# Attention's output projection by seven block products, one weight sum formed by an accumulating transfer

## The chip, the cores and the metric

One core of a Trainium2 chip runs the kernel. The metric is device time in microseconds (us), the median of several runs of the same kernel; lower is better. Engines are named as the profile names them: PE is TensorE's matmul, PEld its weight loads, DVE is VectorE, ACT is ScalarE, POOL is GpSimd, and SP issues most DMAs. L1286 is line 1286 of the kernel before.

## The reference

One inference step of a one-layer trunk over T = 520 token columns (512 of a prompt, 8 decode tokens), model width 2048, everything in float32:

```
y = mixer(rmsnorm(x)); x += y @ w_out          # two recurrent head groups
q = rmsnorm(x) @ w_cq                          # 4 heads of 512, 256 memory tokens
o = softmax(q mk^T / sqrt(512)) mv
x += o @ w_co                                  # 2048 x 2048: attention's output projection
x += relu(rmsnorm(x) @ w_up)^2 @ w_down        # 2048 -> 8192 -> 2048
out = rmsnorm(x)
```

The decode tokens attend to their own cached K and V. The change is about `o @ w_co`.

## The kernel before

Activations lie transposed, 128 features by 520 tokens in a block; a 2048-wide activation is 16 blocks. Every float32 operand is split into a rounded high part and the remainder; a product is three matmuls, high by high, high by low, low by high. A matmul takes a 128 x 128 piece of weights and 260 tokens. Weights come in tiles of 128 x 1024 (512 KB); a "job" is what PE does with one such tile.

The work is a list of jobs run by `run_jobs`. While job i is emitted, the tile of job i+2 is split (ACT writes `whi`, L129 or L138; DVE subtracts to make `wlo`, L130 or L146), tiles further ahead are loaded, and every background task (`start`, `step_tasks`) takes a step. `whi` and `wlo` have three buffers each, so a split waits for the end of the job three before it. In some ranges (`manual_schedule`) each engine keeps the order in which the code was written; elsewhere a planner orders instructions by priority and by its own costs. The attention part and the first four jobs of the w_co projection are in such a hand-ordered range.

Two ways of multiplying are used. `gemm` is the plain one: 48 matmuls a job, and 32 jobs for a 2048 x 2048 projection. `quad_jobs` takes a 2 x 2 arrangement of weight tiles A11, A12, A21, A22 and does seven products in place of eight, each of 24 matmuls. DVE forms four sums of tiles for a group of seven: S3 = A11 - A21, S1 = A21 + A22, S2 = A11 - S1 and the operand of P3, A12 - S2 (L1256). The activations need combinations too: blocks 4 to 7 of an activation pair are made by four DVE subtractions (`block_sums`, L1195, or in `y_sums`), split, and partly parked in DRAM for later loads. Before, w_out (the mixer's projection), w_up and w_down use `quad_jobs`: w_out as one plain pair of output blocks (`out_plain`, four jobs) and seven groups (`out_quad`, 49 jobs). Here w_co is a plain `gemm` over 16 output blocks through `residual`: 32 jobs.

Attention ends per head in `attn_prompt`. The products p @ mv (L222) come four to a head; ACT and DVE split each into `oh`, `ol` (L1159, L1160), which w_co reads. Between them run the jobs that make memory keys and values (`mk_jobs`, L1050; `mv_jobs`, L1081), and the decode tokens' attention, which DVE does by long multiply-reduce instructions (L962, L969) on K and V streamed over POOL's queue (L930, L937).

`residual` loads the old x from DRAM, adds PSUM (L871), stores the new x, and calls `fact_out`, which at once makes the split operands of w_up (`fa`, L800, L801) and the four block combinations, spread over the projection's 16 outputs. `block_loads` then brings the parked ones back. w_up starts with four plain jobs (`up_plain`, L1329), then groups of seven (L1286).

Of the kernel before, what the change touches and what calls it, by code (L numbers as in the profile page):

```python
# [9 lines left out]
F32 = mybir.dt.float32  # L10
F32R = mybir.dt.float32r
# [34 lines left out]
def tile_trunk(ctx: ExitStack, tc: tile.TileContext, a, o):  # L46
# [9 lines left out]
    early_pools = ctx.enter_context(ExitStack())  # L56
    small = early_pools.enter_context(tc.tile_pool(name="small", bufs=2))
    pmm = early_pools.enter_context(tc.tile_pool(name="pmm", bufs=2, space=PSUM))
    paux = early_pools.enter_context(tc.tile_pool(name="paux", bufs=4, space=PSUM))
# [744 lines left out]
    def y_out(t, n):  # L804
        fy[n] = [pair_slot("fy") for _ in range(2)]
        for hf in range(2):
            split_to(fy[n][hf], t[:, HALF[hf]])
        if n % 2 == 0:
            y_even[n // 2] = t
        else:  # L810
            start(y_sums(n // 2, y_even.pop(n // 2), t))

    def y_sums(i, t0, t1):

        yield
        r = stream((P, 4, HT))
        b12, b11, b21, b22 = t0[:, HALF[1]], t0[:, HALF[0]], t1[:, HALF[0]], t1[:, HALF[1]]
        for k, p, q in ((0, b12, b11), (2, b22, r[:, 0]), (1, b22, b12), (3, b21, r[:, 2])):
            V.tensor_tensor(out=r[:, k], in0=p, in1=q, op=ALU.subtract)
        if i >= len(ydram):  # L820
            ykept[i] = {j: r[:, j - 4] for j in range(4, 8)}
            return
        yield
        hi = small.tile([P, 4, HT], F32R, tag="kv", name=nm("kv"), bufs=7)
        S.copy(hi, r)  # L825
        V.tensor_tensor(out=r.bitcast(F32R), in0=r, in1=hi.bitcast(F32), op=ALU.subtract)
        for b, x in enumerate((hi.bitcast(F32), r)):
            load(ydram[i][:, :, b].rearrange("j p c -> p j c"), x)
# [29 lines left out]
    def residual(wname, acts, src, dst, key, out, then=None):  # L858
        js = []
        for n in range(KB):  # L860
            box = {}

            def pre(n=n, box=box):
                box["x"] = xr_tile()
                load(box["x"], src[n])

            def ev(ps, n=n, box=box):
                if n == 0:
                    st[key] = slot(key)
                x1 = slot("x1")  # L870
                V.tensor_tensor(out=halves(x1), in0=ps, in1=halves(box["x"]), op=ALU.add)  # L871
                load(dst[n], x1)
                out(x1, n)
                add_sq(st[key], x1, n == 0)
                if n == KB - 1:
                    start(rstd_task(key))
                    if then:
                        then()
            js += gemm([a[wname][n, g] for g in range(2)], acts, ev, pre)
        return js  # L880


    SC = 512.0 ** -0.5
    xatt, oact = [None] * KB, []
# [210 lines left out]
    def attn_prompt(h):  # L1095
# [57 lines left out]
        ops = []  # L1153
        for j in range(6):
            if j >= 2:
                op = ops.pop(0)
                hi, lo = slot("oh", dt=F32R), slot("ol", dt=F32R)
                for src, c in ((op, slice(0, TP)), (od[:, 4 * h + j - 2], DEC)):
                    S.copy(hi[:, c], src)  # L1159
                    V.tensor_tensor(out=lo[:, c], in0=src, in1=hi[:, c].bitcast(F32), op=ALU.subtract)  # L1160
                oact.append((hi, lo))
# [40 lines left out]
    put_off = []  # L1202

    def fact_out(x1, n):
        if "sb" not in late:
            put_off.append((x1, n))
            return
        fact[n] = [pair_slot("fa") for _ in range(2)]
        for hf in range(2):
            split_to(fact[n][hf], x1[:, HALF[hf]], pc(C_FFN, n))  # L1210
        i, kp = divmod(n, 2)
        if kp == 0:
            tkept[i] = late["sb"].tile([P, 8, HT], F32, tag="r", name=nm("r"), bufs=2)
        r = tkept[i]
        if kp:
            S.activation(r[:, 2:4], halves(x1), AF.Copy, scale=pc(C_FFN, n))
            block_sums(r)
            if i < len(td):
                start(sums_out(tkept.pop(i), i))
            else:  # L1220
                tkept[i] = {j: r[:, j] for j in range(4, 8)}
        else:
            for hf in range(2):
                S.activation(r[:, 1 - hf], x1[:, HALF[hf]], AF.Copy, scale=pc(C_FFN, n))
# [10 lines left out]
    def quad_jobs(srcs, acts, nacc, evac, order=None, early=False):  # L1235
# [82 lines left out]
    def plain_pair(srcs, facts, post):  # L1318
# [3 lines left out]
        def mm(mp, kp, wh, wl):  # L1322
            if kp == 0:
                ps[mp] = mm_tile()
            for j in range(8):
                x = facts[2 * j + kp]
# [29 lines left out]
    x1 = [None] * KB  # L1356

    def x1_load(m):
        for n in (2 * m, 2 * m + 1):
            x1[n] = slot("x1") if m else xr_tile()  # L1360
            load(x1[n], a["xT"][n])

    def x1_done(n):
        load(dx[0][n], x1[n])
        if n == 0:
            st["ssx"] = slot("ssx")
        add_sq(st["ssx"], x1[n], n == 0)
        if n == KB - 1:
            start(rstd_task("ssx"))
        if n >= KB - 2:  # L1370
            xatt[n] = split(x1[n], "xa", pc(C_X, n))

    def x1_again():

        raw = {}
        for n in range(0, KB, 2):
            for k in (n, n + 1):
                if k < KB - 2:
                    raw[k] = slot("x1")
                    load(raw[k], dx[0][k])  # L1380
            if n:
                for k in (n - 2, n - 1):
                    xatt[k] = split(raw.pop(k), "xa", pc(C_X, k))
            yield

    def out_plain():
        def post(mp, ps):
            V.tensor_tensor(out=halves(x1[mp]), in0=ps[:, :, 0:HT], in1=halves(x1[mp]), op=ALU.add)
            x1_done(mp)
            if mp:  # L1390
                x1_load(1)
        js = plain_pair(a["w_out"][0], fy, post)
        js[0]["pre"] = lambda: x1_load(0)
        js[1], js[2] = js[2], js[1]
        return js

    def out_quad(m):
        def evac(p, ps):
            n, hf = dict(P1=(0, 0), P2=(0, 0), P6=(0, 1), P5=(1, 1), P7=(1, 1), P3=(0, 1), P4=(1, 0))[p]
            x = x1[2 * m + n][:, HALF[hf]]  # L1400
            V.tensor_tensor(out=x, in0=ps[:, 0, 0:HT], in1=x, op=ALU.add)
            if p == "P5" and m + 1 < KB // 2:
                x1_load(m + 1)
            if p in ("P3", "P4"):
                x1_done(2 * m + n)
            if p == "P4" and m == KB // 2 - 2:
                start(x1_again())
        return quad_jobs([a["w_out"][m, mp, kp] for mp in range(2) for kp in range(2)],
                         lambda p: [ty[k][PLACE[p]] for k in range(KB // 2)], 1, evac, early=True)
# [151 lines left out]
    jobs += out_plain()  # L1561
    for m in range(1, KB // 2):
        jobs += out_quad(m)
# [11 lines left out]
    jobs += residual("w_co", oact, dx[0], dx[1], "ssf", fact_out, lambda: start(block_loads(tact, fact, td, tkept), 2.0))  # L1575
    jobs[n_early + 1], jobs[n_early + 2] = jobs[n_early + 2], jobs[n_early + 1]
# [21 lines left out]
    early_pools.close()  # L1598
    late["sb"] = ctx.enter_context(tc.tile_pool(name="late", bufs=2, reuse_waits="tile"))
    late["mm"] = ctx.enter_context(tc.tile_pool(name="lmm", bufs=3, space=PSUM, reuse_waits="tile"))  # L1600
    late["aux"] = ctx.enter_context(tc.tile_pool(name="laux", bufs=2, space=PSUM, reuse_waits="tile"))
    for x1, n in put_off:
        fact_out(x1, n)
# [6 lines left out]
def _pack(i):  # L1610
# [6 lines left out]

    i = {k: np.asarray(v) for k, v in i.items()}
    f = np.float32
    par = np.zeros((P, NPAR), f)  # L1620
    for base, name in ((C_MIX, "g_mix"), (C_X, "g_xattn"), (C_FFN, "g_ffn"), (C_FIN, "g_final"),
# [33 lines left out]
        w_out=i["w_out"][0].reshape(8, 2, P, 8, 2, P).transpose(3, 4, 1, 2, 0, 5), w_cq=gran(i["w_cq"][0]), w_co=gran(i["w_co"][0]),  # L1655
        w_up=i["w_up"][0].reshape(8, 2, P, 32, 2, P).transpose(3, 4, 1, 2, 0, 5),
# [49 lines left out]
```

## Time and profile before

| | us |
|---|---|
| median of 3 runs | 2667.88 (2666.63 to 2674.22) |
| profiled execution | 2668.74 |
| its span, first to last instruction | 2667.0 |
| PE busy | 2639.8 |
| DVE busy | 2135.2 |
| ACT busy | 1253.2 |
| granted TensorE clock | 0.998 of full speed |

A busy time is the sum over an engine's instructions. Instructions of one engine overlap a little, so spacing between starts is shorter than the durations shown. The chain of waits is the profile's list, in order of time, of what each moment of the span was spent on, followed back from the last instruction.

### The profile page before, as it was taken

How to read it: one execution, taken by the hardware profiler on the slowest of the kernel's cores; microseconds unless marked ns; L12 is line 12 of the kernel's file. 1: busy time of each engine (PE TensorE's matmuls, PEld its weight loads, DVE VectorE, ACT ScalarE, POOL GpSimd, SP SyncE). 2: the span in 40 equal slices, each digit the busy share in tenths (PEclk: the TensorE clock that was granted, in tenths of full speed). 3: DMA queues.
4: the chain of work that ended last, by engine and by line, in shares of the span. 5: the costliest groups of instructions: out<-in, count | busy, mean ns of one | idle time of the engine just before them, and what ended most of it. 6: DMA issues, size and time to landing. Idle time of an engine off the chain costs nothing.

```text
span 2667.0 us, 52574 instructions
## 1 busy us (share of the span) xinstructions
PE 2639.8 (99%) x21418; PEld 2602.9 (98%) x21418; DVE 2135.2 (80%) x3593; ACT 1253.2 (47%) x1704; POOL 108.3 (4%) x184
## 2 busy tenths in 40 slices
PE   9999999999999999999999999999999999999997
PEld 9999999999999999989999999999999999999997
DVE  6786786897865567775569999999999998998898
ACT  5646364553453144444445555555553333333344
POOL 0010000000001212110000000000000000000001
PEclk9999999999999999999999999999999999999999
DMA  5354443566456778775566565565579666555642
GB/s 205 105 191 135 124 162 105 177 220 235 141 180 200 274 264 279 264 243 192 184 226 228 195 211 196 190 210 198 189 245 335 217 219 219 180 172 191 212 131 89
DMA packets 236068, 528.91 MB, mean 198 GB/s; under 512 B 24638, under 2 KB 96990, under 8 KB 235826
## 3 DMA queue, kind: packets, MB, share of 16 engines
q1 hardware_dynamic: 216882, 458.43, 51.1%
q0 software_dynamic: 18944, 67.12, 7.3%
q8 instruction: 168, 2.75, 0.4%
q14 instruction: 74, 0.61, 0.1%
HBM read 426.27 MB, written 99.33 MB: 197 GB/s over the span
## 4 chain that ended last, share of the span: by engine, by line
PE 91%; issue 4%; DVE 2%; DMA 2%; ACT 1%; POOL 0%; SPq 0%; POOLq 0%; DVEq 0%; ACTq 0%
PE mm L1286 46%; PE mm L203 29%; PE mm L1050 3%; PE mm L1081 3%; PE aux L222 3%; PE aux L1286 2%; PE mm L1329 2%; DVE wlo L130 1%; PE aux L657 1%; DMA wraw<-in_w_in 1%; PE aux L728 0%; PE aux L661 0%; DMA hc<-r 0%; PE aux L654 0%; DMA wraw<-in_w_mv 0%
## 5 line engine op out<-in xcount | busy, mean ns | idle before, releaser
L129 ACT CAST whi<-wraw 128x1024 fp32r<-128x1024 f32 x396 | 416.0, 1051 | 730.1 <-PE mm L1286 388.2
L1286 PE MATMUL mm<-ha,whi 128*128 128x260 f32 x3584 | 643.5, 283 | 1.9 <-ACT whi L129 1.0
L130 DVE TENSOR_TENSOR wlo<-wraw,whi 128x1024 fp32r<-128x1024 f32 x396 | 483.1, 1220 | 151.3 <-ACT whi L129 149.2
L1286 PEld LDWEIGHTS mm<-ha,whi 128*128 128x128 f32 x3584 | 551.0, 188 | 2.8 <-DVE X L1455 1.3
L1286 PE MATMUL mm<-ha,wlo 128*128 128x260 f32 x1792 | 505.0, 282 | 0.6 <-DVE wlo L130 0.6
L1286 PE MATMUL mm<-ta,whi 128*128 128x260 f32 x2320 | 419.3, 283 | 0.0
L1286 PEld LDWEIGHTS mm<-ta,whi 128*128 128x128 f32 x2320 | 356.2, 188 | 0.0
L1286 PEld LDWEIGHTS mm<-ha,wlo 128*128 128x128 f32 x1792 | 337.0, 188 | 1.0 <-DVE wlo L130 1.0
L1286 PE MATMUL mm<-ta,wlo 128*128 128x260 f32 x1160 | 326.8, 282 | 0.0
L1286 PE MATMUL mm<-fa,whi 128*128 128x260 f32 x1488 | 268.3, 282 | 0.0
L203 PE MATMUL mm<-xh,whi 128*128 128x260 f32 x1280 | 264.2, 287 | 0.9 <-DVE og L775 0.9
L203 PE MATMUL mm<-xl,whi 128*128 128x260 f32 x1280 | 259.9, 284 | 0.0
L203 PE MATMUL mm<-xh,wlo 128*128 128x260 f32 x1280 | 257.8, 282 | 0.0
L1286 PEld LDWEIGHTS mm<-fa,whi 128*128 128x128 f32 x1488 | 228.1, 188 | 0.0
L129 ACT CAST whi<-A 128x1024 fp32r<-128x1024 f32 x126 | 132.3, 1050 | 185.6 <-PE mm L1286 120.2
L138 ACT CAST whi<-wraw 128x1024 fp32r<-128x1024 f32 x100 | 105.1, 1051 | 243.5 <-PE mm L203 84.6
L1286 PEld LDWEIGHTS mm<-ta,wlo 128*128 128x128 f32 x1160 | 218.4, 188 | 0.0
L1286 PE MATMUL mm<-fa,wlo 128*128 128x260 f32 x744 | 209.2, 281 | 0.0
L1455 DVE TENSOR_TENSOR X<-mm,X 128x260 f32<-128x260 f32 x448 | 170.6, 421 | 41.4 <-PE mm L1286 39.5
L203 PEld LDWEIGHTS mm<-xh,whi 128*128 128x128 f32 x1280 | 198.4, 188 | 2.3 <-ACT kv L825 1.0
L203 PEld LDWEIGHTS mm<-xh,wlo 128*128 128x128 f32 x1280 | 198.5, 189 | 0.2
L203 PEld LDWEIGHTS mm<-xl,whi 128*128 128x128 f32 x1280 | 198.0, 189 | 0.3
(420 smaller groups left out, 5093.9 us busy)
## 6 DMA issues: line engine op xcount, KB each, us to landing
ha<-hc SPq DMA_DIRECT2D x224, 260.0 KB
wraw<-in_w_in SPq DMA_DIRECT2D x80, 512.0 KB
wraw<-in_w_up SPq DMA_DIRECT2D x66, 512.0 KB
wraw<-in_w_down SPq DMA_DIRECT2D x64, 512.0 KB
A<-in_w_down SPq DMA_DIRECT2D x64, 512.0 KB
A<-in_w_up SPq DMA_DIRECT2D x62, 512.0 KB
hc<-hhi SPq DMA_DIRECT2D x32, 910.0 KB
hc<-r SPq DMA_DIRECT2D x32, 910.0 KB
```

Of the source, the lines that this page charges most:

```text
L129: S.copy(hi, raw)
L130: V.tensor_tensor(out=lo, in0=raw, in1=hi.bitcast(F32), op=ALU.subtract)
L138: S.copy(hi, raw)
L203: PE.matmul(ps[:, hf, 0:HT], w[:, j, :], x[:, HALF[hf]], start=(k == 0 and wi == 0), stop=(k == n - 1 and wi == 2))
L222: PE.matmul(out, u, v, start=first and i == 0, stop=last and i == 2)
L657: PE.matmul(nps[:, ms], C[j][:, ms], qs[j][:, cs], start=False, stop=(j == 1))
L1050: PE.matmul(box["ps"], w[:, i, :], x, start=(k == 0 and wi == 0), stop=(k == KB - 1 and wi == 2))
L1081: PE.matmul(box["ps"][:, i], x[:, ms], w[:, j], start=(k == 0 and wi == 0), stop=(k == KB - 1 and wi == 2))
L1286: PE.matmul(out, w[:, j, :], x[:, b], start=(new and k == 0 and wi == 0), stop=(p == LAST[acc] and k == per - 1 and wi == 2), skip_group_c ...
L1329: PE.matmul(ps[mp][:, hf, 0:HT], w[:, j, :], x[hf][:, b], start=(kp == 0 and j == 0 and wi == 0), stop=(kp == 1 and j == 7 and wi == 2))
L1455: V.tensor_tensor(out=x, in0=c, in1=x, op=ALU.add)
```

## The change

`residual` is gone. A function `projection` now serves both w_out and w_co: four plain jobs for the first two output blocks, then seven groups of seven products. For w_co:

- `attn_prompt` copies each head block to a float32 tile `o` (ACT), and `block_out` splits it into halves `fo`. Blocks are renumbered so that heads 0 and 1 make pairs 0 to 3, and heads 2 and 3 pairs 4 to 7; the rows of w_co are permuted to match on the host.
- For pairs 0 to 3, `o_sums` forms four block differences (DVE), splits them in two steps, and stores them in DRAM over POOL's queue. For pairs 4 to 7, `o_loads` forms and splits the differences, two pairs a step, in the two plain jobs after the tasks have drained; it also loads the stored ones.
- The pool of late SBUF tiles opens after the second w_co job and no longer after the fourth, and the tile loads of the first group are issued there.
- In w_co's groups (`by_dma`), S1 is no DVE instruction: after S3 has read A21, POOL issues a DMA that adds A22 from DRAM onto A21.
- New x blocks are stored, and all but the last two are read back by a task in the last group, which makes `fa` there. The block combinations for w_up (`fact_pair`) stay spread, one pair after each group.

```diff
+    def o_sums(i, t0, t1):
+        yield
+        u, w = slot("ou", (P, 2, HT)), slot("ou", (P, 2, HT))
+        block_diffs(u[:, 0], u[:, 1], w[:, 0], w[:, 1], t0, t1)
+        for k, t in ((0, u), (2, w)):
+            yield
+            hi = pair_slot("oh")
+            S.copy(hi, t)
+            V.tensor_tensor(out=t.bitcast(F32R), in0=t, in1=hi.bitcast(F32), op=ALU.subtract)
+            for b, x in enumerate((hi.bitcast(F32), t)):
+                stream_load(odram[i][k:k + 2, :, b].rearrange("j p c -> p j c"), x)
+    def o_loads():
...
+        for j in (6, 4, 5, 7):
+            if j in (6, 4):
+                for i, t0, t1 in o_last[0:2]:
+                    u, w = slot("ou", (P, 2, HT)), slot("ou", (P, 2, HT))
+                    block_diffs(u[:, 0], u[:, 1], w[:, 0], w[:, 1], t0, t1)
+                    for k, x in ((6, w[:, 0]), (4, u[:, 0]), (5, u[:, 1]), (7, w[:, 1])):
+                        to[i][k] = pair_slot("to")
+                        split_to(to[i][k], x)
+                del o_last[0:2]
+            for i in range(len(odram)):
+                to[i][j] = pair_slot("to")
+                load(to[i][j].bitcast(F32), odram[i][j - 4])
+            yield
...
             if p == "P1":
                 q["S3"] = tt(raw2("S3"), q["A11"], q["A21"], ALU.subtract)
+                if by_dma:
+                    G.dma_start(q["A21"], srcs[3], accum_op=ALU.add)
                 return q["A11"]
...
             if p == "P6":
-                q["S1"] = tt(q["A21"], q["A21"], q["A22"], ALU.add)
+                q["S1"] = q["A21"]
+                if not by_dma:
+                    tt(q["A21"], q["A21"], q["A22"], ALU.add)
                 q["S2"] = tt(q["A11"], q["S1"], q["A11"], ALU.subtract)
...
-    jobs += residual("w_co", oact, dx[0], dx[1], "ssf", fact_out, lambda: start(block_loads(tact, fact, td, tkept), 2.0))
-    jobs[n_early + 1], jobs[n_early + 2] = jobs[n_early + 2], jobs[n_early + 1]
+    jobs += projection("w_co", dx[0], dx[1], "ssf", fo, to, x2_done, fact_split, False)
...
+    early_sb.close()
+    late["sb"] = ctx.enter_context(tc.tile_pool(name="late", bufs=2, reuse_waits="tile"))
+    for fetch in held:
+        fetch()
+    start(o_loads())
+    with tc.manual_schedule():
         run_jobs(n_early + 2, n_early + 4, True)
```

## Rows read from the trace of the kernel before

**Rows 1.** The page: engines' busy us; one costly group (busy, mean ns, idle before).
```profile
PE 2639.8 (99%) x21418; PEld 2602.9 (98%) x21418; DVE 2135.2 (80%) x3593; ACT 1253.2 (47%) x1704; POOL 108.3 (4%) x184
...
L129 ACT CAST whi<-wraw 128x1024 fp32r<-128x1024 f32 x396 | 416.0, 1051 | 730.1 <-PE mm L1286 388.2
```

**Rows 2.** Chain of waits around w_co: start us, us, what.
```profile
1170.35 11.49 PE mm L203 x96
1181.84 5.56 PE aux L222 x24
1187.40 172.01 PE mm L203 x1440
1359.40 5.75 PE mm L1329 x48
```

**Rows 3.** Chain of waits around w_out, its groups' first and last jobs of 49.
```profile
590.09 22.96 PE mm L1329 x192
613.05 2.88 PE mm L1286 x24
...
750.99 2.86 PE mm L1286 x24
753.86 5.77 PE mm L203 x48
```

**Rows 4.** Stretches in w_out, w_co, w_up: us, busy PE, PEld, DVE, ACT, POOL, clock, DMA, GB/s.
```profile
660.00:680.00 20.00, 20.00 (x170) 20.00 (x168) 16.59 (x21) 8.31 (x10) 0.00 (x0) 1.00 0.50 160
1200.00:1220.00 20.00, 20.00 (x170) 20.00 (x169) 11.49 (x18) 8.78 (x15) 0.00 (x0) 1.00 0.61 194
1440.00:1460.00 20.00, 20.00 (x170) 20.00 (x170) 18.33 (x24) 11.04 (x13) 0.00 (x0) 1.00 0.62 212
```

**Rows 5.** DVE in order of time, a w_up group: start us, us, what.
```profile
1445.52 0.42 DVE L1195 TENSOR_TENSOR r<-r 128x260 f32<-128x260 f32 x1
1445.86 1.22 DVE L1256 TENSOR_TENSOR wraw<-wraw,wraw 128x1024 f32<-128x1024 f32 x1
...
1449.15 1.22 DVE L1256 TENSOR_TENSOR S<-wraw,A 128x1024 f32<-128x1024 f32 x1
1450.29 0.42 DVE L1421 TENSOR_TENSOR r<-mm,r 128x260 f32<-128x260 f32 x1
...
1455.19 1.22 DVE L1256 TENSOR_TENSOR A<-A,A 128x1024 f32<-128x1024 f32 x1
1456.33 1.22 DVE L130 TENSOR_TENSOR wlo<-A,whi 128x1024 fp32r<-128x1024 f32 x1
...
1460.12 1.22 DVE L1256 TENSOR_TENSOR wraw<-A,wraw 128x1024 f32<-128x1024 f32 x1
```

**Rows 6.** Landing times of POOL's 512 KB loads (instructions of tile kv, 940:1190).
```profile
DMA to landing us min/median/max: 3.8/7.0/10.5
```

**Rows 7.** Chain of waits in the memory-key jobs after head 1's products.
```profile
1070.51 2.79 PE aux L222 x12
1073.30 22.75 PE mm L1050 x192
1096.06 2.83 PE aux L222 x24
```

**Rows 8.** DVE in order of time, the same jobs (bracket: idle before).
```profile
1081.73 1.22 DVE L146 TENSOR_TENSOR wlo<-wraw,whi 128x1024 fp32r<-128x1024 f32 x1
1082.87 0.42 DVE L1058 TENSOR_TENSOR mk<-mm,rm 128x256 f32<-128x256 f32 x1
1083.20 1.22 DVE L146 TENSOR_TENSOR wlo<-wraw,whi 128x1024 fp32r<-128x1024 f32 x1
...
1086.03 0.43 DVE L1037 TENSOR_TENSOR mkl<-mk,mkh 128x256 fp32r<-128x256 f32 x1 [0.39 <-ACT mkh L1036]
...
1089.08 1.29 DVE L232 TENSOR_TENSOR qal<-q,qah 128x512 fp32r<-128x512 f32 x2 [1.10 <-ACT qah L231]
```

**Rows 9.** SP, DVE, ACT in order of time, where w_co starts.
```profile
1186.82 0.80 SPq L1244 DMA_DIRECT2D A<-in_w_up  x2
1189.41 1.22 DVE L146 TENSOR_TENSOR wlo<-wraw,whi 128x1024 fp32r<-128x1024 f32 x1
1185.79 0.20 ACT L1159 CAST oh<-od 128x8 fp32r<-128x8 f32 x1 [1.92 <-DVE od L969]
1201.50 1.68 DVE L801 SCALAR_TENSOR_TENSOR fa<-x,par,fa 128x260 fp32r<-128x260 f32 x4
```

**Rows 10.** DVE in order of time, w_out's last group: first and last of 16 splits.
```profile
739.16 0.75 DVE L235 SCALAR_TENSOR_TENSOR xal<-x,par,xah 128x520 fp32r<-128x520 f32 x1
739.84 0.42 DVE L1401 TENSOR_TENSOR x<-aux,x 128x260 f32<-128x260 f32 x1
...
760.82 0.76 DVE L235 SCALAR_TENSOR_TENSOR xal<-x,par,xah 128x520 fp32r<-128x520 f32 x1 [0.56 <-ACT xah L234]
```

More of the change, by code (lines that the diff above doesn't have):

```diff
@@ L54, in tile_trunk @@
     dram = ctx.enter_context(tc.tile_pool(name="dram", bufs=1, space=DRAM))
[L56 to L59, printed above, removed]
+    early_sb, early_ps = (ctx.enter_context(ExitStack()) for _ in range(2))
+    small = early_sb.enter_context(tc.tile_pool(name="small", bufs=2))
+    pmm = early_ps.enter_context(tc.tile_pool(name="pmm", bufs=2, space=PSUM))
+    paux = early_ps.enter_context(tc.tile_pool(name="paux", bufs=4, space=PSUM))
     late = {}
@@ L810, in y_out, with block_diffs, pair_sums @@
         else:
-            start(y_sums(n // 2, y_even.pop(n // 2), t))
-    def y_sums(i, t0, t1):
+            start(pair_sums(n // 2, y_even.pop(n // 2), t, ydram, ykept))
+    def block_diffs(d1, d3, d2, d4, t0, t1):
+        b12, b11, b21, b22 = t0[:, HALF[1]], t0[:, HALF[0]], t1[:, HALF[0]], t1[:, HALF[1]]
+        for out, p, q in ((d1, b12, b11), (d2, b22, d1), (d3, b22, b12), (d4, b21, d2)):
+            V.tensor_tensor(out=out, in0=p, in1=q, op=ALU.subtract)
+    def pair_sums(i, t0, t1, td_, kept):
         yield
         r = stream((P, 4, HT))
[L817 to L821, printed above, removed]
+        block_diffs(r[:, 0], r[:, 1], r[:, 2], r[:, 3], t0, t1)
+        if i >= len(td_):
+            kept[i] = {j: r[:, j - 4] for j in range(4, 8)}
             return
@@ L856, in tile_trunk @@
     dx = [[dram.tile([P, T], F32, name=f"dx{i}_{n}") for n in range(KB)] for i in range(2)]
[L858 to L880, printed above, removed]
@@ L883, in tile_trunk, with block_out @@
-    SC = 512.0 ** -0.5
-    xatt, oact = [None] * KB, []
+    SC = 512.0 ** -0.5
+    xatt = [None] * KB
+    fo = [None] * KB
+    to = [[None] * 8 for _ in range(KB // 2)]
+    odram = [dram.tile([4, P, 2, HT], F32, name=f"od{i}") for i in range(KB // 4)]
+    o_even, o_last = {}, []
+    def block_out(t, n):
+        fo[n] = [pair_slot("fo") for _ in range(2)]
+        for hf in range(2):
+            split_to(fo[n][hf], t[:, HALF[hf]])
+        if n % 2 == 0:
+            o_even[n // 2] = t
+        elif n < 8:
+            start(o_sums(n // 2, o_even.pop(n // 2), t))
+        else:
+            o_last.append((n // 2, o_even.pop(n // 2), t))
@@ new lines, in o_loads @@
+    def o_loads():
+        for i in range(KB // 2):
+            to[i][1], to[i][2], to[i][3] = fo[2 * i][0], fo[2 * i + 1][0], fo[2 * i + 1][1]
+        for j in (6, 4, 5, 7):
[11 more added lines that the diff above has]
+            yield
@@ L1152, in attn_prompt @@
         mv = [x[1:] for x in mvx[h]]
-        ops = []
-        for j in range(6):
-            if j >= 2:
-                op = ops.pop(0)
[L1157 to L1161, printed above, removed]
+        ops, parts = [], []
+        for j in range(7):
+            for t, n in parts:
+                block_out(t, n)
+            parts.clear()
+            if 2 <= j < 6:
+                op = ops.pop(0)
+                t = slot("o")
+                S.copy(t[:, 0:TP], op)
+                S.copy(t[:, DEC], od[:, 4 * h + j - 2])
+                parts.append((t, 8 * (h // 2) + 2 * (j - 2) + h % 2))
             if j < 4:
@@ L1200, in tile_trunk, with fact_split, fact_pair @@
     tkept = {}
[L1202 to L1207, printed above, removed]
+    def fact_split(x, n):
         fact[n] = [pair_slot("fa") for _ in range(2)]
         for hf in range(2):
[L1210 to L1221, printed above, removed]
-        else:
-            for hf in range(2):
-                S.activation(r[:, 1 - hf], x1[:, HALF[hf]], AF.Copy, scale=pc(C_FFN, n))
+            split_to(fact[n][hf], x[:, HALF[hf]], pc(C_FFN, n))
+    def fact_pair(i, x0, x1):
+        yield
+        r = late["sb"].tile([P, 8, HT], F32, tag="r", name=nm("r"), bufs=2)
+        for hf in range(2):
+            S.activation(r[:, 1 - hf], x0[:, HALF[hf]], AF.Copy, scale=pc(C_FFN, 2 * i))
+        S.activation(r[:, 2:4], halves(x1), AF.Copy, scale=pc(C_FFN, 2 * i + 1))
+        yield
+        block_sums(r)
+        if i < len(td):
+            start(sums_out(r, i))
+        else:
+            tkept[i] = {j: r[:, j] for j in range(4, 8)}
     def sums_out(r, i):
@@ L1373, in x1_again @@
[L1373 to L1389, printed above, removed]
-            if mp:
[L1391 to L1395, printed above, removed]
@@ L1397, in out_quad, with projection, x_load, x_done @@
-    def out_quad(m):
-        def evac(p, ps):
+    def projection(wname, src, dst, key, facts, tacts, done, again, early):
+        xs = [None] * KB
+        def x_load(m):
+            for n in (2 * m, 2 * m + 1):
+                xs[n] = slot("x1") if m else xr_tile()
+                load(xs[n], src[n])
+        def x_done(n):
+            load(dst[n], xs[n])
+            if n == 0:
+                st[key] = slot(key)
+            add_sq(st[key], xs[n], n == 0)
+            if n >= KB - 2:
+                again(xs[n], n)
+            if n % 2:
+                done(n // 2, xs[n - 1], xs[n])
+            if n == KB - 1:
+                start(rstd_task(key))
+        def read_back():
+            raw = {}
+            for n in range(0, KB, 2):
+                for k in (n, n + 1):
+                    if k < KB - 2:
+                        raw[k] = slot("x1")
+                        load(raw[k], dst[k])
+                if n:
+                    for k in (n - 2, n - 1):
+                        again(raw.pop(k), k)
+                yield
+        def plain_post(mp, ps):
+            V.tensor_tensor(out=halves(xs[mp]), in0=ps[:, :, 0:HT], in1=halves(xs[mp]), op=ALU.add)
+            x_done(mp)
+            if mp:
+                x_load(1)
+        def evac(m, p, ps):
@@ L1408, in out_quad @@
-        return quad_jobs([a["w_out"][m, mp, kp] for mp in range(2) for kp in range(2)],
-                         lambda p: [ty[k][PLACE[p]] for k in range(KB // 2)], 1, evac, early=True)
+                start(read_back())
+        js = plain_pair(a[wname + "0"], facts, plain_post, lambda kp, j: 8 * kp + j)
+        js[0]["pre"] = lambda: x_load(0)
+        js[1], js[2] = js[2], js[1]
+        for m in range(1, KB // 2):
+            js += quad_jobs([a[wname][m, mp, kp] for mp in range(2) for kp in range(2)],
+                            lambda p: [tacts[k][PLACE[p]] for k in range(KB // 2)], 1,
+                            lambda p, ps, m=m: evac(m, p, ps), early=early, by_dma=not early)
@@ L1411, in up_quad, with x_split, x2_done @@
+        return js
+    def x_split(x, n):
+        xatt[n] = split(x, "xa", pc(C_X, n))
+    def x2_done(i, x0, x1):
+        start(fact_pair(i, x0, x1))
+        if i == KB // 2 - 1:
+            start(block_loads(tact, fact, td, tkept), 2.0)
     def up_quad(i):
@@ L1560, in tile_trunk @@
         jobs += gemm(w_in(32 + i), xact, ev_og(i))
-    jobs += out_plain()
-    for m in range(1, KB // 2):
-        jobs += out_quad(m)
+    jobs += projection("w_out", [a["xT"][n] for n in range(KB)], dx[0], "ssx", fy, ty,
+                       lambda i, x0, x1: None, x_split, True)
     for h in range(4):
@@ L1574, in tile_trunk @@
     n_early = len(jobs)
[L1575 to L1576 removed]
+    jobs += projection("w_co", dx[0], dx[1], "ssf", fo, to, x2_done, fact_split, False)
+    held = [jobs[n_early + 4 + i].pop("fetch") for i in range(2)]
+    for i in range(2):
+        jobs[n_early + 4 + i]["fetch"] = lambda: None
     for i in range(PRE):
@@ L1616, in gran, with quads @@
         return w.reshape(k // 1024, 8, P, n // P, P).transpose(3, 0, 2, 1, 4)
+    def quads(w):
+        return w.reshape(8, 2, P, w.shape[1] // 256, 2, P).transpose(3, 4, 1, 2, 0, 5)
     i = {k: np.asarray(v) for k, v in i.items()}
     f = np.float32
+    w_out = i["w_out"][0]
+    w_co = i["w_co"][0].reshape(2, 2, 4, P, D).transpose(0, 2, 1, 3, 4).reshape(D, D)
     par = np.zeros((P, NPAR), f)
```

38 lines of the change are left out of this document (10 added, 28 removed).

## The prediction

> **What bounds the kernel now.** I read the page first, then the chain of waits around w_co and around w_out, then DVE in order of time at the places that the change loads. The page says PE is busy for 99% of the span [rows 1]; that is only a modelled busy time, so the chain decides. Around w_co the chain is PE and nothing else: 96 matmuls in 11.49 us, head 3's products, then 1440 matmuls in 172.01 us up to the first w_up job, with no other engine between [rows 2]. So a matmul removed here is time removed, about 0.12 us each, as long as the other engines keep up. DVE is the one to watch: it is busy 11.5 us of 20 in w_co, but 16.6 in w_out and 18.3 in w_up, where groups of seven run, and PE shows no gap in either [rows 3, 4].
>
> **What it removes from PE.** Before: 32 jobs of 48 matmuls, 11.49 + 172.01 = 183.50 us [rows 2]. After: four plain jobs and seven groups of seven jobs with 24 matmuls, the shape that w_out has already. There the plain jobs took 22.96 us and the 49 jobs ran from 613.05 to 753.85, 140.80 us [rows 3]. Together 163.76. The gain at most is 183.50 - 163.76 = 19.7 us. It is certain as a count (1536 matmuls to 1368); everything below is what is given back. Four places.
>
> **1. The groups themselves.** DVE's instructions overlap, so I use spacing: 1.14 us for a 1024-wide one (1455.19 to 1456.33) and 0.34 for a 260-wide one (1445.52 to 1445.86) [rows 5]. A group has 7 `wlo` and 3 weight sums (S1 is gone), 10 x 1.14 = 11.4; 7 evacuations and 4 combinations for w_up, 11 x 0.34 = 3.7; two sums of squares, under 0.7 each; one 1040-wide remainder, about 1.2. That is 17.7 of a group's 20.1 us (140.80 / 7); by full durations 19.5. Spacing is the nearer one, since w_up at 18.3 busy of 20 keeps PE full [rows 4]. So DVE does not bind, and taking S1 off it brings nothing here beyond slack: 0.
>
> The accumulating transfer is the new wait. The trace has none. It starts when S3 has read A21 and must have landed before S2; behind S2 on DVE stand the `wlo` of the next jobs. In w_up S3 ends at 1450.37 and S2 starts at 1460.12, since S2 overwrites A11 and must follow P1's split: 9.7 us of cover [rows 5]. After that the split is ready well ahead of PE: it starts two jobs, 5.7 us, before use [rows 3], and a 1.05 us cast [rows 1] and a 1.2 us subtraction leave 3.4. So a landing up to about 13 us costs PE nothing. Nearest rows: plain 512 KB loads on POOL's queue land after 3.8 to 10.5 us, median 7.0 [rows 6]. Adding onto bytes that lie there should cost more; the end above is twice the median, 14. I take 8 to 10, hidden, with 1 us in all for small collisions; the ends are 0 and 7 x (14 - 13) = 7.
>
> The median of 7.0 us is what decides the chance of the rival below [rows 6]. The Trainium skill (DMA: Bandwidth & Descriptors, Anatomy of one DMA) fits a POOL-issued transfer as 2.0 us plus bytes over 436 GB/s, an estimate of 3.2 us for 512 KB. The rows are at twice that. By the page that rival would have almost no chance, and the sum would stay.
>
> **2. The attention part.** For pairs 0 to 3 `o_sums` adds DVE work inside the memory-key jobs after head 1's products. There PE runs eight jobs in 22.75 us, 2.84 us each, from 1073.30, without a gap [rows 7]. DVE's order is fixed by hand, and each `wlo` is made two jobs ahead: the one at 1083.20 ends at 1084.4 for the job that starts at 1073.30 + 5 x 2.84 = 1087.5, 3.1 us early; the one at 1081.73 ends at 1082.9 for 1084.7, 1.8 us early [rows 7, 8]. That is all the slack. The new work per pair is 4 differences, 4 x 0.34, and two 520-wide remainders of about 0.6: 2.6 us, 10.4 for four pairs, and because three of them start within two steps it falls on five jobs: about 2.1 (with the last block's own remainders, which now come a step later), 3.3, 3.2, 1.8 and 0.6 us. DVE's idle time there is 0.4 and 1.1 us [rows 8]. Walking through the jobs, DVE falls behind by 11.0 - 1.5, about 2 of it is absorbed by the slack, and 7.5 us arrive at PE. Old and new splits of the blocks themselves weigh the same on DVE. I take 7. From below 2 (if the tasks fall into later, lighter jobs), from above 10 (no slack used, and POOL's 4 MB of stores in the way of key loads). PE is on the chain on both sides, so it isn't won back.
>
> **3. The start of w_co.** PE reaches the third plain job at 1187.40 and has two jobs, 11.5 us, in hand, then P1: P2's weights are due at 1201.8. Before, DVE was done with head 3 and made a `wlo` at 1189.41 [rows 9]. Now each block of head 3 takes two more casts on ACT behind a wait that ends at 1185.79 [rows 9]; I put the last remainder at about 1191.5. A21 can be loaded from 1186.8, when SP's first late tiles went out [rows 9], and isn't later than that. Then in hand-written order: S3 1.1, two pairs of `o_loads` (8 x 0.34 each) 5.4, P1's `wlo` 1.1, an evacuation 0.6, two more pairs 5.4, P2's `wlo` 1.1: 1206.2, so 4.4 us late. PSUM's first late tile may also wait for the second plain evacuation. I take 5. From below 2 (DVE free at 1189.4), from above 9 (every small remainder waits for its cast, and the PSUM wait is real).
>
> **4. The end of w_co.** The last group starts 20.1 us before its end and carries 28 half-block splits, 0.42 each [rows 9], 11.8 us, besides its own 17.7 less the remainder. w_out's last group did the like with 16 splits up to 761.6, 27.8 us after its start at 733.7, and PE did not wait [rows 3, 10], but there the next job read blocks 0 to 7 first. Now the first w_up job reads all even blocks, block 12 at 20.1 + 6/8 x 5.75 = 24.4 us. With some 2 us more DVE work than w_out had, that split lands at about 27 to 28: 3 us. From below 0 (even blocks go first), from above 6.
>
> **The sum.** -19.7 + 1 + 7 + 5 + 3 = -3.7. The profiled execution took 2668.74, 0.86 over the median of the runs; 2665.0 for it, 2664.1 for the median. I forecast 2664 us. Under 0.3%, 8.0 us, is what a measurement here can't tell from no change, so this is "same"; its own range is 2658 to 2672.
>
> **Rivals.**
> *The stalls stay within slack.* Same places at their low ends, 0 + 2 + 2 + 0 to 1: -19.7 + 5 = -14.7, 2653. For it: w_out's last group, which looked overfull on DVE, cost PE nothing [rows 3, 10]. Against: the hand-written order leaves only 1.8 to 3.1 us in the key jobs [rows 8].
> *The accumulating transfer lands too late.* It decides at 13 us and costs 7 us per further us, since every group pays. To be slower than now by 8 it takes about 15 us; at 16 the time is 2664 + 20 = 2684. For it: 10.5 us are seen for plain loads, and DVE waits in order. Against: the median, and 9.7 us of cover [rows 5, 6].
> *DVE's three pile-ups at their upper ends.* 10 + 9 + 6 and 3 for the groups: -19.7 + 28 = +8, 2676. For it: DVE is full in each; against: all three must go wrong.
>
> **Chances.** Forecast 0.46, low-end stalls 0.32, late transfer 0.10, pile-ups 0.12. So faster 0.32, same 0.46, slower 0.22. The range that leaves out 2 in 10 runs from just under the first rival to between the last two: 2652 to 2680.
>
> **What would show it.** Chain of waits after: 192 matmuls in about 23 us, then jobs of 2.87 us. Step 1: no idle time of DVE ahead of S2, and landings of in_w_co on POOL's queue under 13 us. Step 2: a gap of PE ahead of L1050 between 1080 and 1100, put down to `wlo`. Step 3: one ahead of the first or second product of the first group. Step 4: one in the first w_up job, put down to `fa`. The prediction is wrong if these gaps are missing (then 2653 or less), or if every group takes more than 20.1 us (then the transfer or DVE binds).

## The result, and the profile after

The changed kernel takes 2673.25 us, median of 20 runs (2671.57 to 2679.17), against 2670.26 for the kernel before in the same jobs, also 20 runs. The ratio is 1.0016, interval 1.001 to 1.0022. That is some 3 to 6 us slower where 3.7 us faster was forecast, and just above the forecast's own range of 2658 to 2672. It lies within the 0.3% called "same", but with 20 runs of each the sign can be told. The profiled execution took 2677.26 us with a span of 2675.5, which is 4 us over its median; where those 4 us lie is shown below.

The page first. PE lost 168 matmuls, as counted [rows 1], and DVE has a larger share of the chain of waits. The page after, with the chain's shares in its last line, and under it the chain's shares before:

```profile
PE 2631.5 (98%) x21250; PEld 2593.0 (97%) x21250; DVE 2212.7 (83%) x3726; ACT 1295.0 (48%) x1781; POOL 125.6 (5%) x207
...
PE 86%; DVE 5%; issue 5%; DMA 2%; ACT 1%; POOL 0%; SPq 0%; POOLq 0%; DVEq 0%; ACTq 0%
```

```profile
PE 91%; issue 4%; DVE 2%; DMA 2%; ACT 1%; POOL 0%; SPq 0%; POOLq 0%; DVEq 0%; ACTq 0%
```

The chain of waits after, around w_co (start us, us, what), answers to [rows 2]. L1358 is a plain job, L1315 a group's product, L1281 a weight sum, L1288 the accumulating transfer:

```profile
1182.12 5.52 PE mm L1358 x46
...
1203.58 0.77 DVE fo L798 x2
1204.35 1.15 DVE S L1281
...
1232.02 10.03 DMA A<-in_w_co
...
1249.49 88.98 PE mm L1315 x743
...
1368.38 2.46 PE mm L1358 x18
```

Where before there were PE rows only, the chain now runs through ACT and DVE from the second plain job on, and through one transfer of 10.03 us. It is PE's alone for 88.98 us from 1249.49: 743 matmuls, 0.120 us each, the pace of w_out's groups [rows 3]. Around the last group and the first w_up job it runs through ACT, DVE and DMA again, and PE waits 0.4 us in that stretch. Worked out from PE's start times, the first group takes 29.2 us, the second 21.7 and each later one 20.07. So from the third group on the groups run full, and nearly all the losses up to w_up lie ahead of that. PE's waits put numbers on it (total us, times, longest us). The memory-key jobs, 1075 to 1110:

```profile
PE mm L1078 <- DVE wlo L146: 5.5, 4, 1.9
```

And 1160 to 1400:

```profile
PE mm L1315 <- DVE wlo L146: 6.0, 1, 6.0
PE mm L1315 <- DVE x L1427: 1.4, 1, 1.4
PE mm L1315 <- DVE xr L1419: 1.2, 1, 1.2
PE aux L222 <- DVE mvl L1065: 0.8, 1, 0.8
PE mm L1358 <- DVE fa L801: 0.4, 1, 0.4
PE mm L1315 <- ACT whi L129: 0.2, 1, 0.2
```

Here `x` is the evacuation of a group's product, `xr` that of a plain job's, `mvl` the low part of head 3's memory values and `fa` w_up's operand. P1 and P2 are a group's first two products. DVE too stood idle there, ahead of S2 in two groups:

```profile
DVE wraw L1281 <- DMA A<-in_w_co: 4.3, 2, 3.3
```

The stretches of these waits (length, busy PE, PEld, DVE, ACT, POOL, granted clock, DMA, GB/s) show DVE full in both, and PE at half clock after the longest gap; 0.68 and 0.97 are means over a row [rows 4]:

```profile
1085.00:1090.00 5.00, 4.87 (x41) 4.66 (x40) 4.96 (x13) 3.51 (x7) 0.00 (x0) 1.00 0.46 171
1090.00:1095.00 5.00, 3.12 (x24) 2.90 (x24) 4.93 (x12) 2.74 (x6) 2.80 (x5) 1.00 0.68 221
1095.00:1100.00 5.00, 4.44 (x24) 4.14 (x24) 4.96 (x13) 2.26 (x4) 2.46 (x4) 0.68 0.85 253
1215.00:1220.00 5.00, 1.34 (x12) 1.13 (x10) 4.97 (x15) 3.90 (x10) 0.00 (x0) 0.97 0.57 198
1220.00:1225.00 5.00, 2.61 (x12) 2.61 (x13) 5.00 (x9) 1.79 (x4) 0.00 (x0) 0.50 0.24 68
1250.00:1338.00 88.00, 88.00 (x739) 88.00 (x738) 80.48 (x108) 47.73 (x56) 4.23 (x5) 1.00 0.79 235
```

A clock of 0.50 is 1.2 GHz of 2.4. It costs after the wait has ended: PE is back at 1222.39, and its next 18 matmuls take until 1226.45, 4.06 us where the pace of 0.120 makes 2.16. The Trainium skill (TensorE: Matmul & The Clock Gate, Part 1) knows just these two levels and ties them to how busy PE has been; the trace agrees, with 0.50 after the gap of 6.0 us and 1.00 from 1250 on.

What holds PE for 6.0 us is read from DVE in order of time (start us, us, line, what; idle before, in brackets):

```profile
1204.27 1.22 DVE L1281 TENSOR_TENSOR S<-wraw,A 128x1024 f32<-128x1024 f32 x1
1205.40 0.42 DVE L817 TENSOR_TENSOR ou<-o 128x260 f32<-128x260 f32 x1
...
1211.09 1.22 DVE L146 TENSOR_TENSOR wlo<-wraw,whi 128x1024 fp32r<-128x1024 f32 x1
1212.23 0.69 DVE L1419 TENSOR_TENSOR xr<-mm,xr 128x520 f32<-128x520 f32 x1
1213.95 1.23 DVE L1281 TENSOR_TENSOR wraw<-A,wraw 128x1024 f32<-128x1024 f32 x1 [1.03 <-DMA A<-in_w_co]
1215.09 0.42 DVE L817 TENSOR_TENSOR ou<-o 128x260 f32<-128x260 f32 x1
...
1221.12 1.22 DVE L146 TENSOR_TENSOR wlo<-wraw,whi 128x1024 fp32r<-128x1024 f32 x1
```

The order is S3, two pairs of sums, P1's `wlo`, an evacuation, then S2 (L1281 at 1213.95), which waits 1.03 us for its transfer, two more pairs, and only then P2's `wlo`. S2 isn't due until a later product. In the code it stands behind the hand-ordered jobs; the planner moved it ahead of the second two pairs, and the prediction's list for this place doesn't have it.

Landing of the accumulating transfer, from POOL's issue, with the seven issues:

```profile
L1288 POOL DMA_DIRECT2D A<-in_w_co x7: 835/847/954, 1206.2 to 1331.8; - x7
...
DMA to landing us min/median/max: 5.4/5.6/10.0
```

Median 5.6 us, no slower than the plain loads of [rows 6] (7.0), which ran in another stretch. The two that somebody waited for are not the typical ones: the first, issued at 1206.2, took 7.7 us (worked out from the trace), and the second 10.0.

**Stages.** Five profiles of the kernel before (two with a longer start, below) and four of the changed one (two with a longer start), with the stages cut at the first matmul of the memory-key jobs, of w_co's plain jobs and of w_up; mean us, and the least and most:

| stage | before | after | difference |
|---|---|---|---|
| start to memory-key jobs | 942.5 (941.3 to 943.9) | 942.5 (941.2 to 945.2) | 0.1 |
| memory-key jobs to w_co | 229.0 (228.5 to 229.9) | 236.2 (235.8 to 236.7) | +7.2 |
| w_co | 189.06 (189.05 to 189.07) | 181.9 (181.4 to 182.3) | -7.2 |
| w_up to the end | 1307.6 (1307.4 to 1308.2) | 1311.5 (1311.2 to 1312.2) | +3.9 |

The sum is +4.0. The first stage holds what made the profiled execution long: it varies by 3 to 4 us in either kernel ahead of all that the change touches, and was long (945.2) where the granted clock was 0.83 in both 0 to 20 and 240 to 260 us, against 1.00 and 0.91 in the profile of before.

### The profile page after: what moved, and what is told of

Same layout as the page of the kernel before. It is cut to its first block, busy times and chain, and to the rows that moved or that the text cites. A ratio compares the mean times of both kernels' runs of the same rounds, so it can differ in the third digit from the quotient of the medians.

```text
span 2675.5 us, 52658 instructions
## 1 busy us (share of the span) xinstructions
PE 2631.5 (98%) x21250; PEld 2593.0 (97%) x21250; DVE 2212.7 (83%) x3726; ACT 1295.0 (48%) x1781; POOL 125.6 (5%) x207
## 4 chain that ended last, share of the span: by engine, by line
PE 86%; DVE 5%; issue 5%; DMA 2%; ACT 1%; POOL 0%; SPq 0%; POOLq 0%; DVEq 0%; ACTq 0%
PE mm L1315 51%; PE mm L203 21%; PE mm L1109 3%; PE aux L222 2%; PE aux L1315 2%; PE mm L1078 2%; PE mm L1358 2%; DVE wlo L130 1%; PE aux L728 1%; PE aux L657 1%; PE aux L661 0%; DMA out_rh<-hs 0%; DMA A<-in_w_co 0%; DMA wraw<-in_w_in 0%; ACT whi L129 0%
## 5 line engine op out<-in xcount | busy, mean ns | idle before, releaser
L1315 PE MATMUL mm<-ha,whi 128*128 128x260 f32 x3584 | 644.6, 283 | 1.5 <-ACT whi L129 1.0
L1315 PEld LDWEIGHTS mm<-ha,whi 128*128 128x128 f32 x3584 | 551.0, 188 | 2.4 <-ACT whi L129 1.2
L1315 PE MATMUL mm<-ha,wlo 128*128 128x260 f32 x1792 | 505.0, 282 | 0.5 <-DVE wlo L130 0.5
L1315 PE MATMUL mm<-ta,whi 128*128 128x260 f32 x2320 | 419.6, 283 | 0.0
L1315 PEld LDWEIGHTS mm<-ta,whi 128*128 128x128 f32 x2320 | 356.7, 188 | 0.0
L1315 PEld LDWEIGHTS mm<-ha,wlo 128*128 128x128 f32 x1792 | 337.3, 188 | 1.0 <-DVE wlo L130 1.0
L1315 PE MATMUL mm<-ta,wlo 128*128 128x260 f32 x1160 | 327.2, 282 | 0.0
L1315 PE MATMUL mm<-fa,whi 128*128 128x260 f32 x1488 | 269.6, 283 | 0.0
L129 ACT CAST whi<-A 128x1024 fp32r<-128x1024 f32 x140 | 147.0, 1050 | 192.2 <-PE mm L1315 132.7
L1315 PEld LDWEIGHTS mm<-fa,whi 128*128 128x128 f32 x1488 | 228.4, 188 | 0.0
L1315 PEld LDWEIGHTS mm<-ta,wlo 128*128 128x128 f32 x1160 | 218.1, 188 | 0.0
L1315 PE MATMUL mm<-fa,wlo 128*128 128x260 f32 x744 | 209.3, 281 | 0.0
```

The lines of the kernel that those rows point to most:

```text
L129: S.copy(hi, raw)
L1315: PE.matmul(out, w[:, j, :], x[:, b], start=(new and k == 0 and wi == 0), stop=(p == LAST[acc] and k == per - 1 and wi == 2), skip_group_c ...
```

## The experiments

Theory A: the accumulating transfer costs the time, because it lands late. Theory B: DVE's added work costs it, the sums of the attention part in the memory-key jobs (step 2) and the last head's at the start of w_co (step 3). Each of the first eight runs is a median of 11; the kernel before took 2669.63 in the jobs of the first four and 2669.91 in those of the rest (33 runs each). Stages are from one profile each.

| run | us | ratio to before, interval | key jobs | w_co | w_up on |
|---|---|---|---|---|---|
| e1_s1_on_dve | 2674.49 | 1.0015 [1.0006, 1.0023] | 237.3 | 182.0 | 1310.9 |
| e2_sums_spread | 2665.54 | 0.9985 [0.9977, 0.9994] | 230.0 | 181.8 | 1309.4 |
| e3_one_pair_a_step | 2673.62 | 1.0015 [1.0007, 1.0024] | 236.9 | 181.1 | 1310.0 |
| e4_both_spread | 2666.67 | 0.9989 [0.998, 0.9998] | 228.0 | 181.7 | 1311.3 |
| e5_spread_s1_on_dve | 2664.68 | 0.9978 [0.9969, 0.9987] | 229.3 | 178.1 | 1312.1 |
| e6_sums_spread_s1_on_dve | 2665.00 | 0.9985 [0.9976, 0.9993] | 230.2 | 184.2 | 1309.8 |
| e7_spread_first_s1_on_dve | 2664.19 | 0.9979 [0.997, 0.9988] | 228.8 | 178.8 | 1312.3 |
| e8_pairs_by_head | 2666.15 | 0.9985 [0.9976, 0.9994] | 230.7 | 182.3 | 1309.7 |

**e1: the transfer taken out.** S1 is formed by DVE in every group.

```diff
-                             lambda p, ps, m=m: evac(m, p, ps), early=early, by_dma=not early)
+                             lambda p, ps, m=m: evac(m, p, ps), early=early, by_dma=False)
```

> The changed kernel with S1 formed by DVE in w_co's groups again, as in w_up, and no accumulating transfer. Theory A (the gain of 19.7 us was spent in two hand-ordered pile-ups on DVE, one among the memory-key jobs and one at the start of w_co): the time stays within 2 us of the changed kernel's 2673, PE's gaps of 6.0 us at the first group's second product and of 0.6 to 1.9 us in the key jobs stay, and only the 1.4 us wait in the second group goes. Rival B (the accumulating transfer costs it: S2 waits for the landing, 3.3 us once on DVE, and its traffic slows other loads): 5 us or more faster than the changed kernel, ratio to before about 0.9995 or less. Rival C (DVE can't carry a group of seven without the transfer): slower by 5 us or more.

Nothing moved as a whole: 1.0015, w_co 182.0 us. The second group's wait is gone, but in the first the wait for `xr` grew from 1.2 to 2.2 us and one for `whi` from 0.2 to 1.3, and PE still waits for P2's `wlo`:

```profile
PE mm L1315 <- DVE wlo L146: 5.2, 1, 5.2
```

Theory A by itself falls. The test is not quite clean, though: S1 takes 1.1 us of DVE in the place of the 1.0 us that S2 waited.

**e2: the sums of the first four pairs spread.** One task goes through them at a step about every second key job, instead of a task for each pair that starts at once.

```diff
-            start(o_sums(n // 2, o_even.pop(n // 2), t))
+            o_todo.append((n // 2, o_even.pop(n // 2), t))
+            if n == 1:
+                start(o_sums_all(), 1.45)
...
+    def o_sums_all():
+        for _ in range(4):
+            while not o_todo:
+                yield
+            yield from o_sums(*o_todo.pop(0))
```

> The changed kernel with the four pairs' differences made by one task, a step in about every second key or value job, and no longer by four tasks that step at once. The same instructions and the same stores. Theory A: the four gaps ahead of L1078 between 1088 and 1106 (5.5 us, and the slower clock after them) mostly go, 5 to 8 us faster than the changed kernel: 2665 to 2668. Rival B' (not the burst but the work as such, or its 4 MB of stores, is what costs): the same time within 2 us, the gaps only elsewhere.

The key jobs are back at 230.0 us, and PE has no gap there; the same stretch as above in one row:

```profile
1080.00:1100.00 20.00, 20.00 (x171) 20.00 (x170) 19.54 (x41) 10.97 (x17) 6.37 (x10) 1.00 0.83 288
```

DVE is nearly as full as in the change (19.54 of 20), so it is not the amount of work but its falling on five jobs in a row that cost the 7 us. The gap at w_co's start stays, 6.2 us. Step 2 is shown.

**e3: one pair of the last head a step instead of two**, meant to let P2's `wlo` in earlier.

```diff
-            if j in (6, 4):
-                for i, t0, t1 in o_last[0:2]:
+            if True:
+                for i, t0, t1 in o_last[0:1]:
...
-                del o_last[0:2]
+                del o_last[0:1]
```

> The changed kernel with one pair a step in o_loads over four steps, and no longer two pairs in each of the first two. Theory A: P2's weights are ready some 8 us earlier (2.8 us less work twice, and the planner's S2 less in the way), the gap of 6.0 us and the half clock after it go, 5 to 9 us faster than the changed kernel: 2664 to 2668. Rival D (the start is late because of the tiles' loads or the PSUM change, not DVE's differences): within 2 us of the changed kernel.

A miss: PE waits 4.7 us for `wlo`, and 2.9 more for the late pairs' casts on ACT. The reason is one row of DVE: with the pairs out of the way, S2 is reached earlier and waits longer for its transfer, still ahead of P2's `wlo` at 1215.38.

```profile
1211.31 1.23 DVE L1281 TENSOR_TENSOR wraw<-A,wraw 128x1024 f32<-128x1024 f32 x1 [4.18 <-DMA A<-in_w_co]
```

So there are two causes side by side there, and taking away one shows nothing.

**e4: e2 and e3 together.**

> Both of the spreadings together. Theory A: the two add, 11 to 16 us faster than the changed kernel, 2657 to 2662, ratio to before 0.995 to 0.997, with the gap in the key jobs under 2 us and the one at the first group under 2 us. Rivals B and D: no better than 2 us over the changed kernel.

A miss too, 2666.67 where 2657 to 2662 was expected: e2's gain is there, e3 adds nothing. P2's `wlo` is still waited for, and S2 for its transfer, longer than in the change:

```profile
PE mm L1323 <- DVE wlo L146: 5.1, 1, 5.1
```

```profile
1201.65 1.23 DVE L1289 TENSOR_TENSOR wraw<-A,wraw 128x1024 f32<-128x1024 f32 x1 [4.64 <-DMA A<-in_w_co]
```

**e5: e2, e3 and e1 together**, so neither two pairs nor a wait for the transfer stands ahead of P2's `wlo`.

> The kernel with both spreadings, and S1 on DVE in all of w_co's groups. With one pair a step the gap at the first group's second product stayed (4.7 us), and there DVE stood 4.2 us at the first group's S2, which the planner had put ahead of P2's split and which waited for the accumulating transfer. Theory A2 (at the start either is enough: the differences of two pairs, or the wait of S2 for the transfer): without both the gap falls to under 2.5 us and the time to 2662 to 2665, 2 to 5 us below the kernel with both spreadings. Rival D (neither is the cause, the tiles' loads or PSUM are): the gap stays over 4 us, same time within 1.5 us.

w_co falls to 178.1 us, 3.6 less than in e4, and the `wlo` wait to 1.9:

```profile
PE mm L1323 <- ACT to L797: 3.3, 2, 3.0
PE mm L1323 <- DVE wlo L146: 1.9, 1, 1.9
PE aux L222 <- DVE mvl L1073: 0.8, 1, 0.8
```

That is 3.2 us less of this wait than in e4: S1 takes 1.1 us of DVE where S2 waited 4.6. What is late next are the last pairs' casts (`to`). The whole is 0.9978.

**e6: e2 and e1 without e3.** Here both pairs stay in a step.

> The kernel with the sums spread, two pairs a step in o_loads as in the change, and S1 on DVE in w_co's groups. Theory A2: the two pairs alone keep the gap at 4 to 6 us, and the time within 2 us of the kernel with the sums spread and the transfer (2665.5). Rival B (the transfer is what costs at the start): 4 us or more faster than that.

w_co takes 184.2 us; PE waits 2.2 us for `xr`, 1.7 for `mvl`, 1.0 for `whi`, and 3.7 for `wlo`, just under the 4 to 6 expected:

```profile
PE mm L1323 <- DVE wlo L146: 3.7, 1, 3.7
...
DVE kv L1005 <- DMA kv<-in_V: 1.2, 1, 1.2
```

Of the 2.4 us by which w_co is longer here than in e2, 1.4 lie ahead of the third plain job, where DVE stood behind one late load of V (second line); the step tested doesn't touch that load. Two pairs alone keep w_co from getting shorter, as S2's wait alone does in e4: w_co falls by more than 1 us only in e5 and e7, where both are gone. S2 itself was never moved behind P2's split with the transfer kept, so its wait was removed only together with the transfer.

**e7: as e5, but the first late group alone has S1 from DVE** (`by_dma=not early and m > 1`).

> Both spreadings, S1 on DVE in the first group alone, the transfer in the other six. Theory A2: the same as with S1 on DVE in all groups, within 1.5 us: in the later groups the transfer is neither gain nor loss. If the transfer spares DVE something that PE feels: 1.5 us or more faster than that kernel; if its waits cost in each group: slower by as much.

Within 0.5 us of e5. In the other groups the transfer is worth nothing that shows in either direction: it is hidden, and what it takes off DVE was slack. e5 and e7 are the best found, some 0.2% faster than the kernel before.

**e8: pairs formed from blocks of one head**, so that head 2's pairs are ready before w_co and head 3's alone come late (w_co's rows keep their order then; with e2, e3's step and e7's transfer).

```diff
-                parts.append((t, 8 * (h // 2) + 2 * (j - 2) + h % 2))
+                parts.append((t, 4 * h + j - 2))
...
+        elif n < 12:
+            start(o_keep(n // 2, o_even.pop(n // 2), t))
```

> The sums spread, S1 on DVE in the first group, and the pairs made of blocks of one head (heads 0 and 1 go to DRAM as before, head 2's two pairs are made and kept during the last value jobs, head 3's two pairs one a step in o_loads), so half of the differences leave the start of w_co, and no product waits for a pair made in the third or fourth step. Theory A2: the gaps at the first group fall under 2 us in all, and the time to 2659 to 2663, ratio to before 0.996 to 0.998. Rival: DVE, full with head 3's reductions between 1180 and 1200, only hands the lateness on to the third plain job, and the time stays at 2664 to 2667.

No gain, w_co 182.3, as the rival had it: the wait moved to the third plain job, 3.3 us for the cast of `fo`.

```profile
PE mm L1379 <- ACT fo L797: 3.3, 1, 3.3
PE mm L1336 <- issue: 2.0, 1, 2.0
PE mm L1336 <- DVE wlo L146: 1.9, 1, 1.9
```

**f1 to f3: both kernels once more**, unchanged, to see which stage differs by more than it varies.

> The kernel before, once more, to see how far its stages vary from one execution to the next. Theory A (the stretch from the first w_up job to the end is slowed by the change): it takes 1307.0 to 1308.5 us here again, 1307.8 in the first profile. Theory B (that stretch varies with the execution): it takes 1309 to 1311 here, as in the kernels with the change. The time ahead of the first memory-key job is 941 plus up to 4 us by either, by how long the granted clock is low at 0 to 20 and 240 to 260 us.

> The kernel before, a third profile, for the spread. Theory A: from the first w_up job to the end 1307.0 to 1308.5 us. Theory B: anywhere from 1307 to 1312.

> The changed kernel once more. Memory-key jobs to the first plain w_co job 236.8 us and from there to the first w_up job 182.2, within 1 us of the first profile each, by all theories. From the first w_up job to the end: Theory A 1310.5 to 1312; Theory B anywhere from 1307 to 1312.

From w_up on the kernel before took 1308.2 and 1307.4 us, the changed one 1311.3. Theory A of these three holds: 3.9 us (means of the table) go with the change, after the last matmul of w_co. The matmuls begun in 100 us of w_up and of w_down (the PE column's x) show that it is pace, with no wait; first the kernel before (f1), then the changed one:

```profile
1400.00:1500.00 100.00, 100.00 (x841) 100.00 (x840) 91.50 (x116) 55.20 (x65) 0.00 (x0) 1.00 0.66 224
2300.00:2400.00 100.00, 100.00 (x839) 100.00 (x838) 89.58 (x125) 36.40 (x36) 0.00 (x0) 1.00 0.57 194
```

```profile
1400.00:1500.00 100.00, 100.00 (x839) 100.00 (x838) 91.38 (x115) 55.17 (x65) 0.00 (x0) 1.00 0.69 237
2300.00:2400.00 100.00, 100.00 (x837) 100.00 (x836) 89.43 (x126) 36.79 (x35) 0.00 (x0) 1.00 0.54 185
```

Two matmuls of 840 at a granted clock of 1.00. Worked out from PE's start times, 168 matmuls of a w_up group take 20.027 us in every profile of the kernel before (one group of the 31 has 20.020), 20.080 in the changed one. e1, e2 and e6 have 20.080 too, e3 20.060, e8 20.073, e4 20.093, e5 and e7 20.113. In w_up's 31 groups that is 1.7 us between the two kernels, and in 30 of w_down's 1.0 (605.05 for 604.07). e2 and e6 take 603.5 there, less than the kernel before, so the pace goes with the program and not with block products as such.

**g1 to g4: PE's stream shifted**, by more matmuls at the very start (14 become 15 or 22), in either kernel.

```diff
-        for _ in range(14):
+        for _ in range(15):
```

> The kernel before with one more matmul at the very start (15 instead of 14 that run while the first loads are on their way), nothing else. Theory P (the pace of PE in the full stretches of w_up and w_down goes by where their instructions lie in PE's stream): 168 matmuls of a w_up group no longer take 20.027 us, but something else between 20.02 and 20.12. Theory Q (it goes by what the change does to buffers or to other engines): 20.027 again.

> The kernel before with eight more matmuls at the very start. Theory P: another pace than 20.027 us for 168 matmuls of w_up, unless eight matmuls happen to fall on the same alignment. Theory Q: 20.027.

> The changed kernel with one more matmul at the very start. Theory P: another pace than its 20.080 us for 168 matmuls of w_up. Theory Q: 20.080. The waits of the key jobs (5.5 us) and at the start of w_co (6.0 and 1.2 us) stay by both.

> The changed kernel with eight more matmuls at the very start. Theory P: another pace than 20.080 us, unless eight matmuls fall on the same alignment. Theory Q: 20.080.

20.027 us in g1 and g2, 20.080 in g3 and g4. Theory P falls: where the instructions lie in PE's stream is not it. The rows of g1 and then g3, with the matmuls of the unshifted kernels, to one:

```profile
1400.00:1500.00 100.00, 100.00 (x842) 100.00 (x841) 91.66 (x116) 55.18 (x65) 0.00 (x0) 1.00 0.67 223
```

```profile
1400.00:1500.00 100.00, 100.00 (x839) 100.00 (x839) 91.50 (x115) 54.83 (x65) 0.00 (x0) 1.00 0.70 235
```

In each kernel the slow steps (124 to 128 ns instead of 114 to 123) fall on the same matmuls of every group, and mostly on other ones in the changed kernel. That fits a cause in which buffers these matmuls read or write, and as well one in what the other engines do at that point of every group. No run moved a buffer alone or the other engines' order alone; it stays open.

## Why the prediction was wrong

The profiles say +4.0 us where -3.7 was forecast, 7.7 apart. Step 3 was 5.5 too cheap, and 3 us were lost in a place that no step had; steps 1 and 2 and what has no name add 1.3, and step 4 was 2.1 too dear.

**PE's work** (-19.7 us). Right as a count, 168 matmuls, and from the third group on the groups run at w_out's pace.

**Step 1, the groups** (+1). Right in size: one wait of 1.4 us, in the second group, behind the one landing of 10.0. The forecast landing of 8 to 10 us was too long for five of seven, and near for the two that mattered (7.7 and 10.0); adding costs nothing that shows over a plain load. The cover was wrong where it counted. 9.7 us was read in a w_up group; in the first group of w_co DVE came to S2 7.4 us after the end of S3 (1205.49 to 1212.92) and waited, and in the second it waited 3.3. The estimate from the Trainium skill (DMA: Bandwidth & Descriptors, Anatomy of one DMA), 3.2 us, is not borne out: the shortest landing was 5.4, and 3.8 among the plain loads.

**Step 2, the memory-key jobs** (+7). Right in place, cause and size: 7.2 us, made of 5.5 of waits for `wlo` and of the lower clock behind them, and e2 takes them back.

**Step 3, the start of w_co** (+5, at most 9). This step failed by its size. Up to P1 the prediction's walk was right: the last remainder of the third plain job was put 4.1 us after that job's start (1191.5 against 1187.40), and came at 1204.35, 4.0 after 1200.3, which is P1's due time of 1211.8 (1212.97 less the wait of 1.21) less two jobs, 11.5. From there to the end of P2's `wlo` it reckoned 14.7 us (1191.5 to 1206.2), and 18.0 came (1204.3 to 1222.3), so P2's weights were 7.7 us late and not 4.4. The prediction took DVE's order as S3, pairs, P1, pairs, P2; the planner put S2 before the second pairs, 1.0 us of waiting for its transfer and 1.1 of work, two thirds of the 3.3. And the gap so made has a price beyond its length, which the prediction left out: PE comes back at half clock, some 2 us (4.06 less 2.16). In all 6.0 + 1.2 + 0.8 + 0.2 of waits, 0.3 in which the weight load sat idle, and 2: 10.5 us. e4 to e6 show that S2's wait and the two pairs each hold P2 back; 3.6 us, a third of it, are won when both go. The other two thirds are read from the waits and were taken back by no run.

**Step 4, the end of w_co** (+3). Too dear: 0.4 us of wait for `fa`, and about as much in the plain jobs behind it (24.7 us from the first w_up job to the first group, 23.9 before). DVE was full (8.00 of 8 from 1352 to 1360), but the planner had the even blocks done nearly in time.

**What no step had: the pace of w_up and w_down** (0 in the sum). 3.9 us are lost after w_co, of which step 4 is 0.9. Of the remaining 3, w_up's groups have 1.7 and w_down's 1.0. The sum has no term for the rest of the kernel, so it stood at no change without a reason. No row of before could show it; its cause is open.

The sum as measured, by stages: -19.7 + 7.2 (step 2) + 12.6 given back inside w_co (10.5 of step 3, 1.4 of step 1, some 0.7 with no name; the parts are from the first profile) + 3.9 = +4.0, against the 3.0 between the medians and 4.0 between the profiles. Of the prediction's signs the gaps in the key jobs, ahead of the first and the second product and ahead of `fa` all came, where they were said to be. One sign of step 1 failed: DVE did stand idle ahead of S2, 1.0 and 3.3 us in the first two groups. The rival of the late transfer, paid in every group, fell: from the third group on a group takes 20.07 us, and e7 against e5 shows the transfer neutral outside the first. What came was nearest to the rival of the pile-ups (2676), with one of them, step 3, above its upper bound and another, step 4, near its lower.

## What to carry to other kernels

Before costing a hand-written order, write down also what a planner may slip in between, above all an instruction that waits for a transfer: behind it stands everything else of that engine. The time that hides a transfer is to be read where the transfer first runs: 9.7 us in a full group were 7.4 in the first one. When two causes hold the same instruction, taking away one shows nothing (e3, e6); take away both before calling either harmless. A gap of PE of several us is to be priced with the half-speed stretch behind it, here 2 us on 6, and a saving that is below 1% needs several profiles of both kernels by stage, since stages that the change doesn't touch moved by 3 to 4 us.

## What the runs showed that was not expected

An accumulating transfer of 512 KB into SBUF lands in 5.4 to 10.0 us, median 5.6, within the range of plain loads on that queue (3.8 to 10.5). The pace of full matmul stretches goes with the program: 20.027 to 20.113 us for 168 matmuls of w_up, the same in each execution to within some ns, and unmoved by a shift of PE's stream.
